# Attention and GLA jobs recut: 64-row products next to one another, softmaxes in pairs

## The chip, the cores and the metric

The kernel runs on one core of a Trainium2 chip. The core has a matrix engine (TensorE, in the profile PE, with its weight loads shown apart as PEld), three engines for elementwise work (VectorE or DVE, ScalarE or ACT, GpSimd or POOL), and a queue engine (SyncE, SP) that starts most transfers from the main memory. Each engine runs its own list of instructions in order, and lists wait for one another by semaphores. The metric is the device time of one execution in microseconds (us).

## The reference

Four transformer layers over 256 tokens of width 1024 in float32. The first two ("block 1", the same form twice) have a mixer with two attentions and a mixture of 16 experts; then a GLA layer and a differential attention layer ("block 2"), each with a larger mixture of 16 experts. What matters here, cut to the products that the change touches:

```
# block 1, global attention: 8 query heads, 2 key heads of 64
sc = einsum('bqgrd,bkgd->bgrqk', qi, k) * 64**-0.5 ; p = softmax(sc) ; o = p @ v
# block 1, dilated attention: 3 groups of 4 heads of 64, windows with dilation 1, 4, 16
sc = einsum('bqhd,bqkhd->bhqk', qi, kg) * scale + bias ; p = exp(sc - lse) ; o = p @ vg
# GLA: 4 heads, 4 chunks of 64 tokens, keys of 128, values of 256
state = dec[..., None] * state + k_c^T v_c ;  o = q_c state
# differential attention: 8 heads, two score sets of 64 rows each
w = softmax(q1 k1 + bias) - lam * softmax(q2 k2 + bias) ;  o = w @ v
```

## The kernel before

Each mixer is a `Flow` (a class of the kernel): projections by weight tiles of 256 columns, each split into a high and a low half (`whi` by ACT at L325, `wlo` by DVE at L335) and multiplied in three products, at L406, 48 matmuls to a `unit`. These fill PE from the start of a mixer to its end. Between them small tasks run as generators: after every 12 matmuls (`TICK`) `Flow.tick` lets each lane ("ada", "att", "scan", ...) take a step, and a task that yields n rests for n ticks. `width=2` lets two tasks of a lane be active at once. `drain` runs what is left of a lane without matmuls between the steps. What the generators write down is then put in order once more by a scheduler of the framework, which moves single instructions within an engine's list.

The tasks that matter:
- `global_job(tt, v)` (scores L1304, softmax L1307 to L1317, transposes L1326, values L1334): one block of 128 queries and one key head. The key head's 64 rows sit in partitions 0 to 63 or 64 to 127. A job makes the scores of four query heads on the same half of the rows, in two banks `s2`, one softmax after the other with a tick between, and transposes after three or four more ticks.
- `dil_job(tt, c)` (scores L1348 with 256 columns and L1353 in 64 x 64 pieces, softmax L1358 to L1366, transposes L1375, values L1383 and L1388): two heads, one on each half of the rows, again one after the other.
- `scan(h)` (state product `kv` at L1616, output product `po` at L1620, state update by DVE at L1625): one GLA head, four chunks, a step in each tick. `kv` contracts over the 64 rows of a chunk, rows 0 to 63 for even chunks, 64 to 127 for odd ones. `po` contracts over 128 rows and fills only 64 of the array's 128 columns. Heads 0 and 1 run side by side a tick apart, heads 2 and 3 later. `tail(h)` then normalises and transposes.
- `job(tt, hp)` of `diff` (scores L1751, softmax L1754 to L1762, transposes L1770, values L1780): two heads on the two halves of the rows, one after the other, with 128 or 256 keys.

A product of float32 operands is two passes on PE, so one such matmul of the program shows as x2 in the trace. In block 1 a lane "ada" also runs, whose DVE work (`adac`, L501) prepares later modulations and must be drained before `residual`, the last part of a mixer. `residual` is followed by `moe`, whose weight tiles are loaded into buffers that the mixer leaves.

Of the kernel before, what the change touches and what calls it, by code (L numbers as in the profile page):

```python
# [19 lines left out]
P = 128  # L20
# [84 lines left out]
def _plan(places, fixed):  # L105
# [9 lines left out]
          (3, 8, _plan([8, 9, 3, "r", 5] + ["r"] * 7 + [4, 6, 10, 7, "yy", 1, 2, 0, "sa", "rows"], FIX2), 14))  # L115
S_BANKS = 3
# [9 lines left out]
def body(ctx: ExitStack, tc: tile.TileContext, A: dict, out: bass.AP, dbg=None):  # L126
# [989 lines left out]
    def block1(l, prev):  # L1116

        with tc.tile_pool(name="gp", bufs=1, reuse_waits="tile") as gp:
            gates[l, 1] = gp.tile([P, D], F32, name="g2")
            es = gp.tile([P, 2, NE], F32, name="es")  # L1120
            with ExitStack() as stack:
# [26 lines left out]
                if prev is None:  # L1148
                    condR = d2.tile([P, KC, 32], F32, tag="pT", name="condR", bufs=4)
# [148 lines left out]
                def global_job(tt, v):  # L1298
                    hs = slice(64 * v, 64 * v + 64)
                    pr = []  # L1300
                    for c in range(2):
                        s2 = ps.tile([P, 2, 256], F32, tag="s2", name="s2", bufs=S_BANKS)
                        for j in range(2):
                            PE.matmul(s2[:, j, :], qT[hs, 2 * c + j, tt * P:(tt + 1) * P], kT[hs, :], start=True, stop=True,  # L1304
                                      skip_group_check=True)
                        nm = sm.tile([P, 2], F32, tag="nm", name="nm")
                        V.tensor_reduce(nm, s2, axis=AX.X, op=OP.max)  # L1307
                        sc = rq[:, tt, 4 * v + 2 * c:4 * v + 2 * c + 2]
                        V.scalar_tensor_tensor(nm, nm, -1.0, sc, op0=OP.mult, op1=OP.mult)
                        p = d2.tile([P, 2, 256], F32, tag="p", name="p", bufs=3)  # L1310
                        sums = sm.tile([P, 2], F32, tag="sums", name="sums")
                        for j in range(2):
                            S.activation(p[:, j], s2[:, j], AF.Exp, scale=sc[:, j:j + 1], bias=nm[:, j:j + 1],
                                         accum_out=sums[:, j:j + 1])
# [7 lines left out]
                    for p in pr:  # L1322
                        pT = d2.tile([P, 4, P], F32, tag="pT", name="pT", bufs=4)
# [7 lines left out]
                    for c, pT in enumerate(pTs):  # L1331
                        for kc in range(2):
                            for h in range(2):
                                PE.matmul(po[64 * h:64 * h + 64, c, :P], va[:, kc, 64 * v:64 * v + 64], pT[:, 2 * h + kc, :],  # L1334
                                          start=(kc == 0), stop=(kc == 1), tile_position=(0, 64 * h),
                                          skip_group_check=True)
                    yield 1
                    osl = (slice(None), slice(2 * v, 2 * v + 2), slice(tt * P, (tt + 1) * P))
# [3 lines left out]
                def dil_job(tt, c):  # L1342
                    pr = []
                    for hf in range(2):
                        hd = 2 * c + hf
                        s2 = ps.tile([P, 512], F32, tag="s2", name="s2d", bufs=S_BANKS)
                        hs = slice(64 * hf, 64 * hf + 64)
                        PE.matmul(s2[:, 0:256], qdT[hs, c, tt * P:(tt + 1) * P], kdT[hs, c, :],  # L1348
                                  start=True, stop=True, skip_group_check=True)
                        for g in (1, 2):  # L1350
                            for a in range(2):
                                ks = slice(tt * P + 64 * a, tt * P + 64 * a + 64)
                                PE.matmul(s2[64 * a:64 * a + 64, 192 + 64 * g:256 + 64 * g], qdT[hs, 2 * g + c, ks],  # L1353
                                          kdT[hs, 2 * g + c, ks], start=True, stop=True, tile_position=(64 * hf, 64 * a),
                                          skip_group_check=True)
                        slope = 2.0 ** (-8.0 * (hd + 1) / 12)
                        p = d2.tile([P, 384], F32, tag="p", name="pd", bufs=3)
# [3 lines left out]
                        V.tensor_tensor_reduce(p, s2[:, :384], p, 1.0, -3.0e38, OP.add, OP.max, mx)  # L1361
                        V.tensor_scalar(mx, mx, -1.0, None, op0=OP.mult)
                        su = sm.tile([P, 1], F32, tag="su", name="su")
                        S.activation(p, p, AF.Exp, bias=mx, accum_out=su)
                        V.reciprocal(su, su)
# [531 lines left out]
```

## Time and profile before

| what | value |
|---|---|
| median of 3 runs | 1644.25 us (1643.98 to 1645.04) |
| the profiled execution | 1644.99 us, span of its records 1643.2 us |
| PE busy in the span | 1464.9 us, 89% |
| DVE busy | 867.5 us, 53% |
| ACT busy | 430.3 us, 26% |
| mean granted clock of TensorE | 0.952 |

The span runs from the first to the last record of the profile; about 1.8 us of the execution lie outside it. Shares are means over stages of different kinds: the mixers lie at about 45 to 275 us, 447 to 670 us, 855 to 1000 us and 1250 to 1387 us, and the expert layers fill the rest.

### The profile page before, as it was taken

To read this page: it belongs to the slowest core of one execution; us is meant where nothing else is said; L and a number is where in the kernel's file an instruction comes from. 1 tells how busy PE (TensorE), PEld (TensorE's weight loads), DVE (VectorE), ACT (ScalarE), POOL (GpSimd) and SP (SyncE) were. 2 spreads that over 40 slices of the span, in tenths; PEclk is the share of its full clock that TensorE was granted. 3 is DMA by queue.
4 is the path that set the end of the run, shared out by engine and by line. 5 is a ranking of instruction groups with operands and counts; after the bars stand their busy time and mean duration, and the time that the engine had idled before them with its cause. 6 is when DMAs were issued, how large, how long until landed. Compare 5 with 4: busy or idle time off the path is not lost. (4 is left out here: it accounts for less than half of the span.)

```text
span 1643.2 us, 22584 instructions
## 1 busy us (share of the span) xinstructions
PE 1464.9 (89%) x9024; PEld 968.6 (59%) x9024; DVE 867.5 (53%) x1678; ACT 430.3 (26%) x729; POOL 132.9 (8%) x140
## 2 busy tenths in 40 slices
PE   4899997998699999599878998999898999999896
PEld 3788896443288899444447695443336988344332
DVE  3788898343798779524363574221126776122214
ACT  1453341111244433111125242010003552101000
POOL 0300002000130000200020001000002002000000
PEclk9999998999799999799989999999998999999898
DMA  9978699994775688899476387999989856999992
GB/s 307 365 245 282 202 312 352 340 308 165 248 252 171 205 294 251 240 367 358 156 241 199 104 290 256 375 376 366 360 306 296 272 204 240 359 367 387 334 387 104
DMA packets 324383, 461.80 MB, mean 281 GB/s; under 512 B 20077, under 2 KB 178285, under 8 KB 324258
## 3 DMA queue, kind: packets, MB, share of 16 engines
q1 hardware_dynamic: 308400, 445.29, 79.0%
q10 hardware_dynamic: 15858, 14.85, 3.5%
q8 instruction: 77, 1.26, 0.3%
q14 instruction: 48, 0.39, 0.1%
HBM read 456.43 MB, written 3.67 MB: 280 GB/s over the span
## 5 line engine op out<-in xcount | busy, mean ns | idle before, releaser
L763 PE MATMUL gu<-w,xg 128*64 128x512 f32 x1536 | 366.6, 597 | 7.3 <-ACT sa L796 6.5
L763 PEld LDWEIGHTS gu<-w,xg 128*64 128x64 f32 x1536 | 111.2, 137 | 218.9 <-issue 203.1
L817 PE MATMUL y<-w,sa 128*64 128x512 f32 x768 | 207.1, 596 | 1.1 <-DVE sa L801 1.1
L335 DVE TENSOR_TENSOR wlo<-w,whi 128x2048 fp32r<-128x2048 f32 (+2 forms) x92 | 183.4, 1997 | 45.3 <-ACT whi L325 42.4
L325 ACT ACTIVATE whi<-w 128x2048 fp32r<-128x2048 f32 (+2 forms) x92 | 157.7, 1726 | 141.0 <-PE acc L406 103.2
L828 DVE TENSOR_TENSOR yy<-y,yy 128x512 fp32r<-128x512 f32 x32 | 22.1, 692 | 197.3 <-ACT yy L827 197.3
L817 PEld LDWEIGHTS y<-w,sa 128*64 128x64 f32 x768 | 60.9, 137 | 107.4 <-issue 101.0
L501 DVE SCALAR_TENSOR_TENSOR adac<-w,ce,adac 128x512 f32<-128x512 f32 x140 | 104.5, 747 | 1.2
L313 PE MATMUL sc<-yy,st 128*128 128x512 f32 x256 | 87.2, 434 | 19.2 <-ACT yy L827 11.0
L313 PE MATMUL pg<-oh,zh 128*128 128x256 f32 x256 | 77.8, 332 | 25.3 <-DVEq L870 21.7
L406 PE MATMUL acc<-hh,whi 128*128 128x256 f32 x608 | 92.5, 294 | 1.7 <-ACT whi L325 1.7
L406 PE MATMUL acc<-hl,whi 128*128 128x256 f32 x608 | 93.0, 288 | 0.0
L827 ACT ACTIVATE yy<-y 128x512 fp32r<-128x512 f32 x32 | 19.1, 597 | 274.4 <-PE y L817 274.4
L406 PE MATMUL acc<-hh,wlo 128*128 128x256 f32 x608 | 87.1, 282 | 0.2 <-DVE wlo L335 0.2
L851 DVE TENSOR_TENSOR x<-x,sc 128x512 f32<-128x512 f32 x112 | 73.3, 681 | 22.0 <-PE sc L313 21.9
L406 PEld LDWEIGHTS acc<-hh,whi 128*128 128x128 f32 x608 | 80.0, 194 | 7.7 <-issue 4.7
L406 PEld LDWEIGHTS acc<-hl,whi 128*128 128x128 f32 x608 | 80.2, 191 | 4.8 <-issue 4.2
L313 PEld LDWEIGHTS pg<-oh,zh 128*128 128x128 f32 x256 | 58.3, 229 | 39.1 <-PEq L870 18.6
L189 POOL TENSOR_TENSOR rs<-ve,mhalf 128x1 f32<-128x1 f32 x24 | 25.3, 1055 | 678.7 <-DVE ve L188 678.7
L313 PEld LDWEIGHTS sc<-yy,st 128*128 128x128 f32 x256 | 42.0, 188 | 63.5 <-ACT yy L827 26.7
L406 PEld LDWEIGHTS acc<-hh,wlo 128*128 128x128 f32 x608 | 77.8, 188 | 2.2 <-issue 1.7
L823 DVE TENSOR_TENSOR yt<-y,g 128x512 f32<-128x512 f32 x32 | 22.0, 688 | 106.5 <-PE y L817 95.4
(375 smaller groups left out, 2196.9 us busy)
## 6 DMA issues: line engine op xcount, KB each, us to landing
w<-in_moe_w_gate_dram SPq DMA_DIRECT2D x64, 1024.0 KB, 12.1
w<-in_moe_w_up_dram SPq DMA_DIRECT2D x64, 1024.0 KB, 14.3
w<-in_moe_w_down_dram SPq DMA_DIRECT2D x128, 512.0 KB, 10.8
w<-in_w_ada_dram SPq DMA_DIRECT2D x47, 1024.0 KB, 6.5
w<-in_w_in_dram SPq DMA_DIRECT2D x40, 1024.0 KB, 6.6
w<-in_w_exp_gate_dram SPq DMA_DIRECT2D x64, 512.0 KB, 8.7
w<-in_w_exp_up_dram SPq DMA_DIRECT2D x64, 512.0 KB, 8.8
w<-in_w_exp_down_dram SPq DMA_DIRECT2D x64, 512.0 KB, 9.1
```

Source lines behind the costliest of these rows:

```text
L189: G.tensor_tensor(dst, ve, mhalf[:, :n], op=OP.pow)
L313: PE.matmul(dst, l, r, start=(i == 0), stop=(i == n - 1), skip_group_check=True)
L325: S.activation(hi[:, k0:k0 + n], w, AF.Copy)
L335: eng.tensor_tensor(lo[:, k0 + x:k0 + y], w[:, x:y], hi[:, k0 + x:k0 + y].bitcast(F32), op=OP.subtract)
L406: PE.matmul(dst, l, r, start=(start and i == 0), stop=(i == n - 1), skip_group_check=True)
L501: V.scalar_tensor_tensor(acc, ws[k // 4][:, k % 4], ce[:, k:k + 1], acc, op0=OP.mult, op1=OP.add)
L763: PE.matmul(gu[64 * j:64 * j + 64, :], xg[:, 4 * kh + k, (2 * pr + j) * CAP:(2 * pr + j + 1) * CAP], ws[j][:, k, :], start=(kh == 0 and k ...
L817: PE.matmul(y[64 * j:64 * j + 64, :], aT[:, f, 64 * j:64 * j + 64], w[:, j, k, :], start=(f == 0), stop=(f == NF - 1), tile_position=(0, 6 ...
L823: V.tensor_tensor(yt[:, hs], y, gate[:, hs], op=OP.mult)
L827: S.activation(yh[:, hs], src, AF.Copy)
L828: V.tensor_tensor(yl[:, hs], src, yh[:, hs].bitcast(F32), op=OP.subtract)
L851: V.tensor_tensor(X[:, tt, hs], X[:, tt, hs], sc, op=OP.add)
```

## The change

The jobs are cut along other lines, so that a product on rows 0 to 63 stands next to one on rows 64 to 127, and in the GLA a product on columns 0 to 63 next to one on columns 64 to 127.
- `global_job` takes a pair of query heads `c` for both key heads instead of four query heads of one key head. The four score products alternate between the halves and between two banks. Both softmaxes' exponentials come before both normalisations, and one wait of four ticks (`SM_TICKS`) stands where there were waits of 1, 1 and 3. A pause of two ticks (`JOB_GAP`) stands between the first two jobs of the lane.
- `dil_job` and `job` write both heads' scores first, alternating the halves, then both softmaxes, then wait four ticks.
- `scan(ha)` runs two heads with the second one chunk behind, in six steps of two ticks.
- The softmax tiles `p` get 4 buffers instead of 3, the transposed tiles `pT` 3 instead of 4.

The number of products, of softmax and of copy instructions stays the same. The core of the diff:

```diff
+SM_TICKS = 4
+JOB_GAP = 2
+P_BUFS = 4
...
-                def global_job(tt, v):
-                    hs = slice(64 * v, 64 * v + 64)
+                def global_job(tt, c):
+                    s2 = [ps.tile([P, 2, 256], F32, tag="s2", name="s2", bufs=S_BANKS) for _ in range(2)]
+                    for j in range(2):
+                        for v in range(2):
+                            hs = slice(64 * v, 64 * v + 64)
+                            PE.matmul(s2[v][:, j, :], qT[hs, 2 * c + j, tt * P:(tt + 1) * P], kT[hs, :], start=True, stop=True,
+                                      skip_group_check=True)
                     pr = []
-                    for c in range(2):
-                        s2 = ps.tile([P, 2, 256], F32, tag="s2", name="s2", bufs=S_BANKS)
-                        for j in range(2):
-                            PE.matmul(s2[:, j, :], qT[hs, 2 * c + j, tt * P:(tt + 1) * P], kT[hs, :], start=True, stop=True,
-                                      skip_group_check=True)
+                    for v in range(2):
...
+                        pr.append((p, sums))
+                    for p, sums in pr:
                         V.reciprocal(sums, sums)
                         for j in range(2):
                             V.tensor_scalar(p[:, j], p[:, j], sums[:, j:j + 1], None, op0=OP.mult)
-                        pr.append(p)
-                        yield 1
-                    yield 3
+                    yield SM_TICKS
...
-                        fl.add("att", *[global_job(tt, v) for tt in range(2) for v in range(2)], width=2)
+                        fl.add("att", global_job(0, 0), pause(JOB_GAP), global_job(0, 1), global_job(1, 0), global_job(1, 1), width=2)
...
-            def scan(h):
+            def scan(ha):
+                heads = (ha, ha + 1)
+                po = {h: ps.tile([P, 2, 256], F32, tag="s2", name="po", bufs=3) for h in heads}
+                for m in range(6):
+                    kv = {}
+                    for h in heads:
+                        n = m - (h - ha)
+                        if 0 <= n < 4:
...
+                            PE.matmul(kv[h][:, :256], kt[rows_, n // 2, h * P:(h + 1) * P], v[rows_, n // 2, h * 256:(h + 1) * 256],
+                                      start=True, stop=True, skip_group_check=True)
...
+                    yield 2
...
-            fl.add("scan", scan(0), scan(1), width=2)
+            fl.add("scan", scan(0), width=2)
...
-                fl.add("scan", scan(2 + u))
+                if u == 1:
+                    fl.add("scan", scan(2))
```

What the scheduler makes of it is seen in PE's list. In the first mixer, at the first global job (`s_843`, `s_870` and so on are score banks, L1304 the score products, L406 the projections), the list before has two products to a bank, each bank on one half of the rows:

```order
L1304 MATMUL s_843<-kT,qT 128x256 x2
L406 MATMUL acc<-hl,whi 128x256 x4
L406 MATMUL acc<-hh,wlo 128x256 x8
L1304 MATMUL s_870<-kT,qT 128x256
L1291 MATMUL ptq<-consts,qro 128x128 x4
L1304 MATMUL s_870<-kT,qT 128x256
L1304 MATMUL s_883<-kT,qT 128x256 x2
```

In the changed program (where all lines of the code stand 3 or more further down) the same place on PE reads:

```order
L1307 MATMUL s_843<-kT,qT 128x256
L1307 MATMUL s_844<-kT,qT 128x256
L1307 MATMUL s_843<-kT,qT 128x256
L1307 MATMUL s_844<-kT,qT 128x256
L409 MATMUL acc<-hl,whi 128x256 x4
L409 MATMUL acc<-hh,wlo 128x256
```

The first job's four products now alternate between a bank of one half and a bank of the other, without a projection between them.

In the GLA, on PE, at the second to fourth chunk of the first heads (`kv` state products, `po` output products, one chunk and one head each), before:

```order
L1616 MATMUL kv<-vg,kq 128x256
L1620 MATMUL po<-st,kq 64x256
L1616 MATMUL kv<-vg,kq 128x256
L1620 MATMUL po<-st,kq 64x256
L406 MATMUL acc<-whi,hl_10488 128x256 x4
L406 MATMUL acc<-wlo,hh_10487 128x256 x8
L1616 MATMUL kv<-vg,kq 128x256
L1620 MATMUL po<-st,kq 64x256
```

And in the changed program at that place:

```order
L1628 MATMUL kv<-vg,kq 128x256 x2
L1634 MATMUL po<-st,kq 64x256 x2
L409 MATMUL acc<-whi,hl_10488 128x256 x4
L409 MATMUL acc<-wlo,hh_10487 128x256 x8
L409 MATMUL acc<-whi,hh_10487 128x256 x8
L409 MATMUL acc<-whi,hl_10488 128x256 x4
```

Two heads' state products stand together, and behind them two heads' output products; the next such group comes 24 projections later.

At the end of the differential attention, on PE, where the last job's scores (`s2f`), transposes (`ptf`) and value products (`podf`) meet the first products of `residual` (`oh`, `ol` are the heads' outputs), before:

```order
L1751 MATMUL s2f<-kq 128x256 x2
L406 MATMUL acc<-wlo,oh_15539 128x256 x6
L406 MATMUL acc<-whi,oh_15539 128x256 x6
L406 MATMUL acc<-whi,ol_15540 128x256 x6
L406 MATMUL acc<-wlo,oh_15539 128x256 x6
L1770 MATMUL ptf<-consts,pbuf 128x128
L1780 MATMUL podf<-vb,wT 128x128
L1770 MATMUL ptf<-consts,pbuf 128x128 x3
```

And in the changed program, from the last scores on:

```order
L1766 MATMUL s2f<-kq 128x256 x4
L409 MATMUL acc<-whi,hl_15538 128x256 x4
L409 MATMUL acc<-wlo,hh_15537 128x256 x8
L409 MATMUL acc<-whi,oh_15539 128x256 x6
L409 MATMUL acc<-whi,ol_15540 128x256 x6
L409 MATMUL acc<-wlo,oh_15539 128x256 x6
L409 MATMUL acc<-whi,oh_15539 128x256 x6
L409 MATMUL acc<-whi,ol_15540 128x256 x6
L1791 MATMUL ptf<-consts,pbuf 128x128 x2
L409 MATMUL acc<-wlo,oh_15539 128x256 x6
L1801 MATMUL podf<-vb,wT 128x128 x2
L1791 MATMUL ptf<-consts,pbuf 128x128 x4
```

Between the last scores and the transposes of the last job stand 48 projections where there were 24.

## Rows read from the trace of the kernel before

**Rows 1.** The page, busy us, share of the span and instructions of each engine.

```profile
PE 1464.9 (89%) x9024; PEld 968.6 (59%) x9024; DVE 867.5 (53%) x1678; ACT 430.3 (26%) x729; POOL 132.9 (8%) x140
```

**Rows 2.** Busy us by stretch of the mixers: stretch, length, engines, granted clock, DMA.

```profile
82.00:205.00 123.00, 121.27 (x958) 104.91 (x957) 105.64 (x206) 50.74 (x86) 0.00 (x0) 0.95 0.73 243
205.00:246.00 41.00, 38.90 (x311) 38.33 (x311) 37.95 (x67) 17.28 (x22) 0.00 (x0) 0.96 0.97 313
500.00:617.00 117.00, 116.79 (x1007) 106.51 (x1006) 93.98 (x189) 53.23 (x89) 0.00 (x0) 1.00 0.70 232
905.00:950.00 45.00, 45.00 (x259) 31.54 (x258) 25.42 (x39) 12.90 (x12) 2.10 (x3) 1.00 0.37 120
1276.00:1348.00 72.00, 72.00 (x556) 66.08 (x555) 53.73 (x183) 44.79 (x107) 4.16 (x6) 1.00 0.68 221
```

**Rows 3.** The longest wait of PE from 82 to 246 us: total, times, longest.

```profile
PE acc L406 <- ACT mh L1458: 2.1, 1, 2.1
```

**Rows 4.** Timeline of PE, first global job: start, us, line, operation, shape, records.

```profile
83.94 1.13 PE L1304 MATMUL s<-kT,qT 64*128 64x256 f32 x4
85.00 0.74 PE L406 MATMUL acc<-hl,whi 128*128 128x256 f32 x4
...
87.83 1.13 PE L1304 MATMUL s<-kT,qT 64*128 64x256 f32 x6
88.89 1.21 PE L406 MATMUL acc<-hh,whi 128*128 128x256 f32 x8
```

**Rows 5.** PE busy (records) of the global scores L1304 alone, by mixer.

```profile
82.00:205.00 123.00, 8.60 (x32) 4.98 (x32) 0.95 0.73 243
500.00:617.00 117.00, 6.79 (x32) 4.09 (x32) 1.00 0.70 232
```

**Rows 6.** Timeline of PE, dilated scores of two heads.

```profile
124.24 0.70 PE L1348 MATMUL s2d<-kdT,qdT 64*128 64x256 f32 x2
124.86 0.45 PE L1353 MATMUL s2d<-kdT,qdT 64*64 64x64 f32 x8
```

**Rows 7.** PE busy of the dilated scores in the second mixer, L1348, then L1353.

```profile
500.00:617.00 117.00, 5.57 (x16) 2.35 (x16) 1.00 0.70 232
...
500.00:617.00 117.00, 3.58 (x64) 2.48 (x64) 1.00 0.70 232
```

**Rows 8.** PE busy in the GLA, of `kv` L1616, then of `po` L1620.

```profile
905.00:950.00 45.00, 11.14 (x32) 4.71 (x32) 1.00 0.37 120
...
905.00:950.00 45.00, 10.33 (x32) 3.06 (x32) 1.00 0.37 120
```

**Rows 9.** Timeline of PE in the GLA, one `po` run.

```profile
916.40 0.65 PE L1620 MATMUL po<-st,kq 128*64 128x256 f32 x2
```

**Rows 10.** The page, costliest group: expert products on alternating column halves.

```profile
L763 PE MATMUL gu<-w,xg 128*64 128x512 f32 x1536 | 366.6, 597 | 7.3 <-ACT sa L796 6.5
```

**Rows 11.** PE busy of the differential scores L1751.

```profile
1276.00:1348.00 72.00, 12.39 (x64) 7.84 (x64) 1.00 0.68 221
```

**Rows 12.** Timeline of PE, four differential score products, 128 and 256 keys.

```profile
1280.93 1.14 PE L1751 MATMUL s2f<-kq 64*128 64x128 f32 x8
```

**Rows 13.** Timeline of PE, end of the differential attention, with idle time and releaser.

```profile
1350.96 0.33 PE L1770 MATMUL ptf<-consts,pbuf 128*128 128x128 f32 x1 [1.17 <-DVE pbuf L1762]
1352.23 0.41 PE L1770 MATMUL ptf<-consts,pbuf 128*128 128x128 f32 x2 [0.94 <-DVE pbuf L1762]
```

**Rows 14.** Busy us of one stretch of the first mixer, columns as in rows 2.

```profile
160.00:170.00 10.00, 10.00 (x62) 7.07 (x61) 4.63 (x15) 1.73 (x6) 0.00 (x0) 0.56 0.37 133
```

**Rows 15.** Softmax of a global job: groups by tile (min/median/max ns), then by line (mean).

```profile
L1313 ACT ACTIVATE p<-s,nm,rq x32: 546/560/566, 90.2 to 530.7; 128x256 f32<-128x256 f32 x32
...
L1307 DVE TENSOR_REDUCE nm<-s x16: 668/681/693, 88.7 to 526.3; 128x2 f32<-128x512 f32 x16
...
L1317 DVE TENSOR_SCALAR p<-p,sums 128x256 f32<-128x256 f32 x16 | 4.9, 346 | 0.0
```

**Rows 16.** Lines of DVE from 82 to 250 us.

```profile
L335 DVE TENSOR_TENSOR wlo<-w,whi 128x2048 fp32r<-128x2048 f32 (+2 forms) x24 | 44.0, 1841 | 6.7 <-ACT whi L325 6.5
```

More of the change, by code (lines that the diff above doesn't have):

```diff
@@ L1493, in bias_task @@
         yield 1
-        fsb = pool.tile([8, 384], F32, tag="pT", name="fsb", bufs=4)
+        fsb = pool.tile([8, 384], F32, tag="pT", name="fsb", bufs=3)
         V.tensor_copy(fsb, pf[0:8, :384])
@@ new lines, in scan @@
+            def scan(ha):
[6 more added lines that the diff above has]
+                        if 0 <= n < 4:
+                            rows_ = slice(64 * (n % 2), 64 * (n % 2) + 64)
+                            kv[h] = ps.tile([P, 512], F32, tag="acc", name="kv", bufs=3)
+                            PE.matmul(kv[h][:, :256], kt[rows_, n // 2, h * P:(h + 1) * P], v[rows_, n // 2, h * 256:(h + 1) * 256],
+                                      start=True, stop=True, skip_group_check=True)
+                    for h in heads:
+                        n = m - (h - ha)
+                        if 0 < n < 5:
+                            i, par = n - 1, (n - 1) % 2
+                            PE.matmul(po[h][64 * par:64 * par + 64, i // 2, :], qT[:, h, i * 64:(i + 1) * 64], st[i % 2][:, h],
+                                      start=True, stop=True, tile_position=(0, 64 * par), skip_group_check=True)
+                    for h in heads:
+                        n = m - (h - ha)
+                        if n == 0:
+                            V.tensor_copy(st[0][:, h], kv[h][:, :256])
+                        elif 0 < n < 4:
+                            V.scalar_tensor_tensor(st[n % 2][:, h], st[(n + 1) % 2][:, h], dec[:, h, n:n + 1], kv[h][:, :256],
+                                                   op0=OP.mult, op1=OP.add)
+                    yield 2
+                for h in heads:
+                    o = og[:, h]
+                    S.activation(o, po[h], AF.Copy)
+                    sq = d2.tile([P, 2, 256], F32, tag="hf", name="sq2", bufs=1)
+                    ss = sm.tile([P, 2], F32, tag="ssd", name="ssg")
+                    V.tensor_tensor(sq, o, o, op=OP.mult)
+                    V.tensor_reduce(ss, sq, axis=AX.X, op=OP.add)
+                    rs2 = sm.tile([P, 2], F32, tag="rsg", name="rsg", bufs=4)
+                    rstd_of(rs2, ss, LN_EPS, 2, 1.0 / 256)
+                    for tt in range(2):
+                        V.scalar_tensor_tensor(o[:, tt], o[:, tt], rs2[:, tt:tt + 1], gn[:, h * 256:(h + 1) * 256], op0=OP.mult, op1=OP.mult)
+                    os[h] = o
+                    yield 1
@@ L1742, in job @@
                 pair = pairs.pop(0)
+                s2 = [ps.tile([P, 512], F32, tag="s2", name="s2f", bufs=S_BANKS) for _ in range(2)]
+                for i in range(2):
+                    for hf in range(2):
+                        rows_ = slice(64 * hf, 64 * hf + 64)
+                        PE.matmul(s2[hf][:, i * 256:i * 256 + nk], qT[hp][rows_, i, tt * P:(tt + 1) * P], kT[hp][rows_, i, :nk],
+                                  start=True, stop=True, skip_group_check=True)
                 for hf in range(2):
                     h = 2 * hp + hf
-                    rows_ = slice(64 * hf, 64 * hf + 64)
-                    s2 = ps.tile([P, 512], F32, tag="s2", name="s2f", bufs=S_BANKS)
                     p = pbuf[:, pair[hf]]
@@ L1750, in job @@
                     for i in range(2):
[L1751 to L1754 removed]
+                        V.tensor_tensor_reduce(p[:, i, :nk], s2[hf][:, i * 256:i * 256 + nk], Tb[h // 4][:, h % 4, 256 - nk:256], 1.0, -3.0e38,
                                                OP.add, OP.max, mx[:, i:i + 1])
@@ L1758, in job @@
                         S.activation(p[:, i, :nk], p[:, i, :nk], AF.Exp, bias=mx[:, i:i + 1], accum_out=su[:, i:i + 1])
+                    ws.append((p, su))
+                for p, su in ws:
                     V.reciprocal(su, su)
```

90 lines of the change are left out of this document (30 added, 60 removed).

## The prediction

> **What bounds the kernel now.** I read the page's engine table first: PE is busy 89% of the span, DVE 53%, ACT 26% [rows 1]. Such a mean hides the stages, so next came the busy time of each engine in the stretches of the mixers where the changed jobs run [rows 2]. There PE stands at 121.27 of 123 us, 116.79 of 117, 45.00 of 45 and 72.00 of 72: in these stretches the time is PE's list, and a microsecond taken out of it is a microsecond of the kernel, as long as the engine behind it keeps up. Third I read PE's waits. Over both stretches of the first mixer the longest costs 2.1 us [rows 3]; none has to do with the products that are recut. DVE is second: 86% in the first stretch, 93% in the next (37.95 of 41), 80% in the second mixer, 56% in the GLA, 75% in the differential attention [rows 2]. So only the first mixer has an engine close behind PE.
>
> Last I read what a product over half the array costs. A float32 product is two passes, two records. Two global score products on one half of the rows take 1.13 us from the first start to the last end, and the next run begins 1.06 after it (83.94 to 85.00). The run at 87.83 holds six records, three products, one of them on the other half; it takes the same 1.13, and again 1.06 to the next run [rows 4]. So a product on rows 0 to 63 and one on 64 to 127 do run at once. One score product alone takes 0.70, 0.62 to the next run [rows 6]. All prices below follow: one step of two passes 0.70, two steps 1.13; every run overlaps the next by 0.07 (1.13 less 1.06).
>
> **The change part by part, in PE's busy time.** The number of products stays; the steps shrink where opposite halves stand together.
>
> Global scores. Now 8.60 us in the first mixer and 6.79 in the second [rows 5]. In the changed list the first mixer has three groups of four products that alternate, and the last job's four cut into two runs of two on one half each: 5 runs x 1.13 = 5.65, a saving of 2.95. The second has three such groups and two runs of one pair: 3 x 1.13 + 2 x 0.70 = 4.79, saving 2.00.
>
> Dilated scores. In the second mixer 5.57 + 3.58 = 9.15 us [rows 7]. All four jobs stand paired there: 0.70 for the two large products, and for the 64 x 64 pieces, now eight products in a run where a run of four takes 0.45 [rows 6], between 0.45 (a run twice as full costs the same) and 0.90 (no gain). The trace shows no such run; I take 0.60, nearer to the rows on which opposite halves overlap. 4 x 1.30 = 5.20 saves 3.95, bounds 2.75 to 4.55. In the first mixer two of the four jobs stand paired; by the same 1.0 a job, 2.0.
>
> Scan. `kv` takes 11.14 and `po` 10.33 us for 16 products each [rows 8], so 0.70 and 0.65 apiece. The changed list has `kv` as 5 pairs and 6 single ones, since the second head runs one chunk behind: 11 x 0.70 = 7.7, saving 3.4. `po` lies on column halves: 6 pairs and 4 single ones. A lone run takes 0.65 [rows 9]. What a pair on column halves gives is read from the expert products, alternating column halves, two passes of 512 columns: 366.6 us for 1536 records, 239 ns each [rows 10], where a pass of 256 columns alone already takes 0.22 (the 0.43 between 1.13 and 0.70, halved). So column halves overlap nearly fully, a pair costs about 0.70, and 4 x 0.65 + 6 x 0.70 = 6.8 saves 3.5. Were column halves not to overlap here, nothing of this 3.5 comes.
>
> Differential scores. 12.39 us [rows 11] in 13 runs of all forms. The changed list has eight groups of four, half of them with 128 keys. A run with two 128-key products on one half and two 256-key ones on the other took 1.14 [rows 12]. So a 256-key group costs 1.13. A 128-key group does half of that, 0.70, and 1.13 at the worst. 4 x 0.70 + 4 x 1.13 = 7.3 saves 5.1 (3.4 at the worst).
>
> These sum to 2.95 + 2.00 + 3.95 + 2.0 + 3.4 + 3.5 + 5.1 = 22.9 us. But busy time of a run contains the 0.07 that the next run overlaps: some 28 runs fewer give back 28 x 0.07 = 2.0. Remain 20.9.
>
> End of the differential attention. Here PE waits 1.17 and 0.94 us for the last softmaxes [rows 13]. The changed list puts 24 more projections ahead of the transposes. One takes (1.21 - 0.74) / 4 = 0.12 us [rows 4], so 2.8 us more cover, against which the joint softmax is later by one softmax's rest. I count a gain of 2, bounds 0 and 3.
>
> Waits that the joint softmax brings. A global job's pair needs maximum 0.68 twice, four exponentials of 0.56, four multiplications of 0.35 [rows 15]; these add to 5.0, and overlap of ACT and DVE brings the chain to about 4.8. Ahead of the transposes stand 52 to 105 projections, 6.2 to 12 us. The least margin is 1.4 us, less than one weight split of DVE (1.84 [rows 16]). Behind a waiting transpose stand all later projections, and behind these the split buffers. Bounds 0 and 4; I count 1.
>
> First mixer. DVE is so near its limit [rows 2] that part of the 4.95 us saved there ends as a wait for splits instead. The wait of 2.1 us [rows 3] shows that this happens today. I count half lost, 2.5; bounds 0 and 5.
>
> Clock. The granted clock is 1.00 in all the stretches but the first mixer's. There it falls to 0.56 in one stretch of 10 us [rows 14], close to the lower level of 1.2 GHz, while the list is dense with transposes and small products. At the full clock these 10 us would be 5.6, so 4.4 to win at most. In the changed list projections stand between those products. Bounds: 4.4 lost once more elsewhere and 4.4 won. I count 1 won.
>
> Copies, softmax and DMAs keep their numbers. One buffer fewer for `pT`, one more for `p`: the DMA of the bias task that takes a `pT` buffer must also wait for DVE, on ACT's queue, behind which ACT's casts stand; the table's use is over 500 us later, so nothing.
>
> Sum: 20.9 + 2 - 1 - 2.5 + 1 = 20.4 us, from the profiled execution's 1645.0 (span 1643.2): 1624.6. The median of the runs shown lies 0.7 lower, so 1623.9: **1624**.
>
> **Rivals.** *DVE becomes the bound in the first mixer and later the split paces PE elsewhere too.* For it: 93% in one stretch. Against: 56% to 80% in the others. All 4.95 of the first mixer go, and a quarter of the other 18: 1624 + 2.5 + 4.5 = 1631. A sentence of the Trainium skill stands beside it (TensorEngine Tiling (Array Packing), section "PSUM Bottleneck"): tiling speeds up the matrix engine but not the emptying of its results. By that rule alone the DVE-bound first mixer gives nothing, which the trace neither shows nor excludes.
>
> *A product's two passes start strictly in the program's order.* Then the second half's first pass can begin only with the first half's second, and every group lasts one pass longer, 0.22 us; with about 27 groups 5.9 us, so 1630. Against it: the six records in the time of four [rows 4] would then take 1.35. The Trainium skill says so (TensorE: Matmul & The Clock Gate, section "Part 3: Packing small matmuls — row/col tiling"): products start and end in program order without reordering. By the rule it is 1630, by the row 1624; the row decides for me.
>
> *Slower: PE blocks at the joint transposes.* Before, the first softmax's transposes needed one softmax through; now both must be. If DVE takes three splits of 1.84 in between, the chain is 4.8 + 5.5 = 10.3 us against leads of 6.2 to 12. Jobs with short leads, some 12 of 24, then wait 2 us each, 24 us in all: 1648. It decides from a chain of 8.3 us on, that is two foreign splits. For it: DVE's load in the first mixer. Against: its 56% to 80% elsewhere, and most leads are longer.
>
> *The pairs don't overlap in the new order* (results go to other banks, weights change each time): only the end and the fewer runs are left, about 1642. Rows 4 speak against it.
>
> *Better: the clock stays up and all bounds go well.* Clock 4.4, no loss on DVE 2.5, no waits 1, end 1 more, small products 0.9: 3.4 + 2.5 + 1 + 1 + 0.9 = 8.8, so 1615.
>
> **How the numbers follow.** Chances: the forecast's case 0.52, DVE as the bound 0.18, order of passes 0.10, blocked transposes 0.07, no overlap 0.05, better 0.08. The range takes in the better case and the two dearer ones with their spread, 1613 to 1636; outside lie the last two cases and the tails. A measurement of this kernel can tell about 0.2%, 3.3 us, from no change. Faster holds all but blocked transposes and half of the no-overlap case: 0.89; same 0.05; slower 0.06.
>
> **What would show it.** Right: a first-job run of eight score records of about 1.13 us, `kv` pairs of 0.70, and PE busy in the five stretches shorter by some 21 us in sum, while the expert layers stay. The order of passes shows as 1.35 for such a run and 0.9 for `kv` pairs. DVE as the bound shows as waits of projections for `wlo` in the first mixer; the blocked transposes as PE's idle time ahead of `ptp`, `ptd` and `ptf`. The forecast is wrong if a run of eight records takes about 2 us, or if over 8 us of new PE idle time appear.

## The result and the profile after

| | median | runs | ratio to the kernel before |
|---|---|---|---|
| before | 1644.55 us | 1643.98 to 1645.04 | |
| after | 1622.38 us | 1619.32 to 1625.64 | 0.9859, 95% interval 0.9842 to 0.9876 |
| forecast | 1624 us | range 1613 to 1636 | |

The kernel became 22.2 us faster, 1.4%. The profiled execution of after took 1619.32 us, its span is 1617.5, 25.7 shorter than that of before. The first part of the page (busy us, share of the span, instructions) answers to [rows 1]:

```profile
PE 1435.8 (89%) x9024; PEld 953.5 (59%) x9024; DVE 864.3 (53%) x1678; ACT 428.6 (26%) x729; POOL 131.4 (8%) x140
```

PE has as many instructions as before and 29.1 us less busy time. The same five stretches as in [rows 2], cut at about the same places in the program (engines PE, PEld, DVE, ACT, POOL, then granted clock, DMA share, GB/s). The cuts are rounded, so that lengths are compared only in the table further down:

```profile
84.00:198.00 114.00, 113.33 (x966) 101.70 (x964) 103.46 (x205) 50.41 (x86) 0.00 (x0) 0.99 0.77 253
198.00:242.00 44.00, 39.48 (x311) 38.27 (x310) 40.39 (x71) 17.34 (x22) 0.00 (x0) 0.96 0.92 307
495.80:607.00 111.20, 110.31 (x1009) 102.76 (x1008) 93.81 (x190) 52.46 (x89) 0.00 (x0) 1.00 0.73 239
886.00:925.00 39.00, 39.00 (x283) 32.24 (x281) 21.66 (x28) 13.62 (x11) 1.40 (x2) 1.00 0.45 157
1256.00:1324.00 68.00, 67.67 (x552) 63.15 (x551) 53.71 (x187) 44.87 (x114) 4.16 (x6) 1.00 0.74 247
```

PE still fills its stretches. Now the recut products alone, as PE busy time (records) by stretch: the global scores (answering to [rows 5]), the dilated scores in 256 columns and in 64 (first and second mixer each, [rows 7]), `kv` and `po` ([rows 8]), the differential scores ([rows 11]):

```profile
84.00:198.00 114.00, 5.66 (x32) 0.99 0.77 253
495.80:607.00 111.20, 4.81 (x32) 1.00 0.73 239
...
84.00:198.00 114.00, 4.19 (x16) 0.99 0.77 253
495.80:607.00 111.20, 2.87 (x16) 1.00 0.73 239
...
84.00:198.00 114.00, 3.36 (x64) 0.99 0.77 253
495.80:607.00 111.20, 1.85 (x64) 1.00 0.73 239
...
890.00:945.00 55.00, 7.87 (x32) 1.00 0.50 172
...
890.00:945.00 55.00, 6.50 (x32) 1.00 0.50 172
...
1256.00:1324.00 68.00, 7.80 (x64) 1.00 0.74 247
```

And PE's timeline (start, us, line, operation, records). A run of eight records is four products, two on each half; four records are two products:

```profile
87.09 1.13 PE L1307 MATMUL s<-kT,qT 64*128 64x256 f32 x8
...
546.39 0.70 PE L1352 MATMUL s2d<-kdT,qdT 64*128 64x256 f32 x4
547.02 0.46 PE L1358 MATMUL s2d<-kdT,qdT 64*64 64x64 f32 x16
...
908.44 0.70 PE L1628 MATMUL kv<-vg,kq 64*128 64x256 f32 x4
909.07 0.65 PE L1634 MATMUL po<-st,kq 128*64 128x256 f32 x4
...
1315.33 0.71 PE L1766 MATMUL s2f<-kq 64*128 64x128 f32 x8
...
1317.81 1.13 PE L1766 MATMUL s2f<-kq 64*128 64x256 f32 x8
```

Four products take what two took [rows 4], two take what one took [rows 6, 9].

For the rest of this text the program is cut at the same instructions of PE's list in every kernel, and a stretch is the time from PE's start of the one to its start of the other, added up from the timeline. "First mixer" runs from the first projection to the products of `residual`, "second mixer" from a projection just ahead of its first global job into its `residual`, "scan" from the GLA's last projections before it to the experts, "end" is the last job of the differential attention and its `residual`. Where a stretch takes in `residual`, it runs up to the routing and the experts' first gather products (`pg`):

| stretch, us | before | after |
|---|---|---|
| first mixer | 201.6 | 196.5 |
| second mixer | 163.8 | 158.0 |
| GLA ahead of the scan | 43.2 | 40.6 |
| scan | 105.7 | 98.0 |
| differential attention | 95.2 | 91.7 |
| its end | 48.4 | 47.1 |
| all else | 985.4 | 985.6 |

(All else is what is left of the span: 1643.2 and 1617.5.) The gain lies where the jobs were recut. In the same way, start to start, the recut products hold PE for 21.9 us less: global 14.4 to 9.8, dilated 17.4 to 10.7, `kv` 10.0 to 7.1, `po` 9.2 to 5.8, differential 11.5 to 7.2.

### The profile page after: what moved, and what is told of

It is laid out like the page before. It is cut to its first block, busy times and chain, and to the rows that moved or that the text cites. A ratio compares the mean times of both kernels' runs of the same rounds, so it can differ in the third digit from the quotient of the medians.

```text
span 1617.5 us, 22578 instructions
## 1 busy us (share of the span) xinstructions
PE 1435.8 (89%) x9024; PEld 953.5 (59%) x9024; DVE 864.3 (53%) x1678; ACT 428.6 (26%) x729; POOL 131.4 (8%) x140
## 5 line engine op out<-in xcount | busy, mean ns | idle before, releaser
L854 DVE TENSOR_TENSOR x<-x,sc 128x512 f32<-128x512 f32 x112 | 73.3, 681 | 22.1 <-PE sc L316 21.9
```

The lines of the kernel that those rows point to most:

```text
L854: V.tensor_tensor(X[:, tt, hs], X[:, tt, hs], sc, op=OP.add)
```

## Experiments

Times are medians. The kernel before stood at 1644.4 to 1645.6 beside them. Totals of the changed program spread by 6 to 11 us between executions, but for one that is named, so that a few us are read from a stretch of the profile and not from the total.

**The changed kernel again.**

> The changed kernel once more, unchanged. Its four times spread from 1619.3 to 1625.6 us, where the kernel before spread by 1.1. Theory: the saved products are the same in every execution, so the score products, kv and po keep their PE busy time (5.7, 4.8, 7.8, 7.1 to 7.8 and 5.8 to 6.4 us), and what varies is the clock and the waits of the start and of the first mixer. Rival: the pairs overlap in some executions only; then the PE busy time of the score products differs from the first profile by over 1 us. Median between 1619 and 1625.

1620.15 us by the median of all six executions. One of them took 6154 us; why is not known. The other five have a median of 1617.97 us (1615.47 to 1624.87), ratio 0.9836 (0.9814 to 0.9859), and from here on this is what is called the second measurement of the changed kernel. All the recut products lie within 0.03 us of the first profile. What differs is elsewhere: the GLA ahead of the scan took 43.0 us where the first profile has 40.6, with a granted clock of 0.91 over 20 us (first line, this run) where the first profile has 1.00 (second fence), and two expert stages took 0.9 and 2.4 us more.

```profile
865.00:885.00 20.00, 19.79 (x130) 17.24 (x130) 9.84 (x7) 14.66 (x18) 0.00 (x0) 0.91 0.51 160
```

```profile
865.00:885.00 20.00, 19.19 (x136) 16.65 (x137) 10.69 (x7) 16.12 (x19) 0.00 (x0) 1.00 0.52 161
```

So the 2.6 us of that stretch in the table are not the change's.

**Order inside the groups.** The loops over halves and over products change places:

```diff
-                    for j in range(2):
-                        for v in range(2):
+                    for v in range(2):
+                        for j in range(2):
```

> The groups of scores are written with both products of one half first and then both of the other (A A B B in place of A B A B), in the global, the dilated and the differential attention; neighbours stay neighbours. Theory N (neighbours): PE takes up the other half's product as soon as its rows are free, whatever the order inside the group; runs of eight records stay at 0.71 (128 keys) and 1.13 us, the time stays within 2 us of the changed kernel, 1622. Rival A (alternation): products start in order, so the second A has to begin before the first B; a group takes three product times in place of two, +0.43 for each of some 10 groups of 256 columns, +0.22 for 4 of 128, about +0.5 for each of 6 dilated jobs: 4.3 + 0.9 + 3 = +8.2 us, 1630.5, and the runs of eight at 1.56.

1621.79 us, ratio 0.9858 (0.9836 to 0.9879). In the global scores and the differential ones order costs nothing; in the dilated ones everything that the pairing had brought is gone. (The list did run in the new order: in single records of the trace the other half's first product starts 13 ns behind the first one of the run at 495.63, and 7 ns behind it in the changed kernel.)

```profile
495.63 1.14 PE L1307 MATMUL s<-kT,qT 64*128 64x256 f32 x8
...
545.99 0.70 PE L1352 MATMUL s2d<-kdT,qdT 64*128 64x256 f32 x2
546.62 0.45 PE L1357 MATMUL s2d<-kdT,qdT 64*64 64x64 f32 x8
547.00 0.70 PE L1352 MATMUL s2d<-kdT,qdT 64*128 64x256 f32 x2
547.62 0.45 PE L1357 MATMUL s2d<-kdT,qdT 64*64 64x64 f32 x8
```

Neither theory holds alone: N where two products of a half stand in a row, A where five do. The second mixer takes 161.7 us, 3.7 more, about what four dilated jobs lose (2.08 from 545.99 to the last end, in place of 1.09 each).

**Small products half by half.** To see why:

```diff
-                    for g in (1, 2):
-                        for a in range(2):
-                            for hf, hs in enumerate(rows_):
+                    for hf, hs in enumerate(rows_):
+                        for g in (1, 2):
+                            for a in range(2):
```

> The dilated scores in the order A256 B256, then four small products of half A, then four of half B. In the second run the order with five products of A ahead of five of B took 2.08 us for 20 records in place of 1.04, while A A B B in the other attentions took no more than A B A B. Theory W (PE finds the other half's product only if it stands no more than two or so products behind): the eight small ones run one after the other, a run takes about 0.7 + 0.9 = 1.5 us. Rival C (a full-width product of half B could not start beside small ones, whose columns are halves; small ones beside small ones can): 1.04 to 1.1 us, as in the changed kernel.

```profile
544.77 0.70 PE L1352 MATMUL s2d<-kdT,qdT 64*128 64x256 f32 x4
545.40 0.47 PE L1358 MATMUL s2d<-kdT,qdT 64*64 64x64 f32 x16
```

1622.47 us, one run. Four small products of one half, then four of the other: they overlap fully, 1.10 us for the job. So W falls: PE finds a partner four products behind. What the run before lacked fits C: there the first product of the other half was a wide one behind small ones that each fill half the columns. C is not shown by itself. In the run before five products of a half stood ahead of the other half's, here four, so that a reach of PE which ends between four and five would fit both runs as well.

**Both heads of the scan on the same chunk.**

```diff
-                        n = m - (h - ha)
+                        n = m
```

> The GLA's two heads run on the same chunk in place of one chunk apart: two kv products stand together on the same half of the rows, two po products on the same half of the columns. The same neighbours, even fewer interruptions of the projections, but no opposite halves. Theory (halves): a kv pair takes 1.13 in place of 0.70 us, a po pair about 1.08 in place of 0.65; kv 7 x 1.13 + 2 x 0.70 = 9.3 against 7.7, po about 8.6 against 6.5, less some 0.8 for fewer interruptions: +3 us, about 1625 if the changed kernel stands at 1622. Rival (grouping): the GLA's gain came from standing in groups and breaking the projections less often; then it is 1 us faster than the changed kernel, 1621, and kv and po together take no more PE time than in it.

1623.64 us, ratio 0.9870 (0.9850 to 0.9889). `kv` and `po` by busy time in the scan, then two of its pairs in the timeline:

```profile
880.00:945.00 65.00, 9.29 (x32) 1.00 0.54 184
...
880.00:945.00 65.00, 8.62 (x32) 1.00 0.54 184
```

```profile
901.50 1.13 PE L1628 MATMUL kv<-vg,kq 64*128 64x256 f32 x4
902.56 1.08 PE L1634 MATMUL po<-st,kq 128*64 128x256 f32 x4
```

As the theory of halves had it (9.3 and 8.6). The scan's stretch is 102.7 us, 4.7 more than changed and 3.0 less than before: standing together is worth something, the halves are worth more. Of the 3.0 us, 2.5 are `kv` and `po` themselves: start to start `kv` goes from 10.0 to 8.65 and `po` from 9.2 to 8.06, since a run's first product costs 0.63 and a second one behind it only 0.43. The projections around them give some 0.6 (71.3 us before, 70.7 here).

**One part undone at a time.** The edits put back the functions of the kernel before, for the first two mixers' jobs, for the scan, for the differential attention's jobs; a line of each:

```diff
-                def global_job(tt, c):
+                def global_job(tt, v):
...
-            fl.add("scan", scan(0), width=2)
+            fl.add("scan", scan(0), scan(1), width=2)
...
-                yield SM_TICKS
+                    yield 1
+                yield 3
```

> The changed kernel with the global and dilated jobs of the first two mixers as before; GLA and differential attention recut. Theory (each part saves in its own stretch, by its own products): the first two mixers take as long as before (first 141, second 164 us, where the changed kernel takes 136.5 and 158), GLA and differential attention as long as changed (98 and 92): 10 to 11 us slower than the changed kernel, 1631 to 1633. Rival (the gain is one of clock and waits that come and go): the second mixer stays within 2 us of the changed kernel's.

> The changed kernel with the GLA's scan as before. Theory (own products): kv 10.0 and po 9.2 us in place of 7.1 and 5.8 by the time from start to start, the scan's stretch at 105.5 in place of 98, 7.5 us slower, 1628 to 1630; the score products and all other stretches as in the changed kernel. Rival (the forecast's price of 0.70 for a po pair was right, and the rest of the gain in the stretch came from the clock): po returns by 2.5 us only and the stretch by 5.

> The changed kernel with the differential attention's jobs as before. Theory (own products; at the end the waits only moved): the scores at 11.5 in place of 7.2 us, the stretch up to the last job's values at 95.1 in place of 91.7, its end at 48.4 in place of 47.1: 4.5 us slower, 1625 to 1627. Rival (the longer cover of 24 more projections is worth the 2 us that were forecast for the end): the end alone at 49 or more.

| stretch, us | before | after | mixers' jobs old | scan old | diff. jobs old |
|---|---|---|---|---|---|
| first mixer | 201.6 | 196.5 | 198.7 | 196.2 | 195.7 |
| second mixer | 163.8 | 158.0 | 163.7 | 157.6 | 157.6 |
| scan | 105.7 | 98.0 | 97.7 | 105.7 | 98.0 |
| differential attention | 95.2 | 91.7 | 91.8 | 91.8 | 95.1 |
| its end | 48.4 | 47.1 | 47.2 | 47.6 | 48.7 |
| median of the runs | 1644.55 | 1622.38 | 1627.93 | 1624.53 | 1623.02 |

In the second mixer, the scan and the differential attention each part gives its own stretch back to within 0.3 us and moves none of the others by more than 0.5: with the scan old, `kv` and `po` stand at 11.14 and 10.33 us busy, the numbers of [rows 8]. Measured from the changed kernel's first median, the totals moved by less than I had expected (5.6, 2.2 and 0.6 us, against 10, 7.5 and 4.5), and from its second by about as much (10.0, 6.6 and 5.1). The two medians of the same program lie 4.4 us apart, so the totals decide nothing here. The first mixer is the exception: its old jobs cost 2.2 us there, not 5.

**One tick less of cover.**

```diff
-SM_TICKS = 4
+SM_TICKS = 3
```

> The changed kernel with three ticks in place of four between both softmaxes and the transposes, 12 projections or 1.4 us less cover. It puts the forecast's slower case to the test (PE blocks at the joint transposes). Theory (cover is ample, chain about 4.8 us): PE's waits ahead of ptp, ptd and ptf stay under 2 us in sum, the time within 3 us of the changed kernel. Rival (the cover is just enough in the changed kernel): most of 24 jobs wait over 0.7 us, 15 to 25 us slower, above 1635.

1623.93 us, ratio 0.9886 (0.9855 to 0.9916). PE waits 0.3 us ahead of `ptf` and nothing that shows ahead of `ptp` and `ptd`. The forecast's slower case is out. What it costs lies elsewhere: the differential attention takes 94.4 us, 2.7 more. PE waits there four times ahead of value products and `pto`, 1.2 us in all (0.2 in after), and its projections are cut into 31 pieces in place of 25; how much of the rest the pieces cost was not tried by itself.

**DVE's load in the first mixer.**

```diff
-            V.scalar_tensor_tensor(acc, ws[k // 4][:, k % 4], ...)
+            if step == 1 or k % 4 == 0: V.scalar_tensor_tensor(acc, ws[k // 4][:, k % 4], ...)
```

> In the first mixer only, the modulation task leaves out six of its eight terms (the output is then not the reference's; its weights are still loaded): some 72 DVE instructions of 0.75 us less, 53 us of DVE work less in the first mixer. Theory (DVE paces the merge stage of the first mixer, 207 to 232 us, and took back what the products saved): PE's waits there for mt (2.3 us) go and the waits for mh (2.1) and behind (1.9, 2.2) shrink: 2 to 6 us faster than the changed kernel, 1616 to 1620. Rival (the waits are ACT's or the latency of the chain's): no more than 0.5 us faster.

The total, 3116.49 us, says nothing: the modulations are other ones, and the stages behind the first mixer take twice the time (probably because the tokens go to other experts; not looked into). The first mixer can still be compared, since its instructions but those left out are the same. It took 179.3 us against 196.5, and its `residual` 41.1 against 49.2. The longest waits of PE from 84 to 280 us (total, times, longest), in after:

```profile
PE pos L707 <- DVE r_m L540: 4.1, 1, 4.1
PE ptq L1294 <- DVE qro L1288: 2.7, 1, 2.7
PE acc L409 <- DVE wlo L338: 2.2, 1, 2.2
PE acc L409 <- ACT mh L1465: 2.1, 1, 2.1
PE accb L409 <- DVE mt L1463: 2.0, 2, 1.5
PE acc L409 <- DVE ot L975: 1.9, 1, 1.9
```

and in this run, where all but the first are gone and that one is shorter:

```profile
PE pos L707 <- DVE r_m L540: 2.3, 1, 2.3
PE rp L1002 <- ACT hTr L996: 1.2, 2, 1.0
PE pg L316 <- DVE oh L723: 1.0, 1, 1.0
PE pa L511 <- DVE pTd L1383: 0.7, 1, 0.7
```

I had expected 2 to 6 us, since I counted only the four waits that begin with `wlo`. It is 25. By PE's list, start to start, 14 of the 25 us are waits of PE (8 of them those four), about 8 are projections that took less time, at a somewhat higher granted clock (0.99 over the mixer in place of 0.97), and 2.7 are recut products, because all jobs stand paired in this list. So DVE's work costs this mixer waits, but not all of the 25 us are waits for DVE.

**The same work on PE.** A generator like the existing tile at the kernel's start makes eight of the twelve modulation tiles; its core:

```diff
+        for k in range(KC):
+            for j in range(4):
+                PE.matmul(pa[32 * j:32 * j + 32, :128], cond[:, k, :], ws[k // 4][:, k % 4, j * 128:(j + 1) * 128],
+                          start=(k == 0), stop=(k == KC - 1), tile_position=(0, 32 * j), skip_group_check=True)
```

> The changed kernel, and in the first mixer 8 of the 12 modulation tiles are made by PE (32 products of 32 columns each, as at the kernel's start) in place of 8 DVE instructions of 0.75 us each: some 45 us of DVE work less in the first mixer, PE some 6 to 8 us more there (0.05 us for a pass, 64 passes, a transposition, less the 1.04 us of the products that go). Theory (DVE paces the first mixer): the fourth run, with 53 us of DVE work less, was shorter by 25 us from the mixer's start to its end; here 18 to 21 come back less 7: 11 to 14 us faster than the changed kernel, 1607 to 1611. Rival (PE paces it, and the fourth run was faster because its DVE results were not needed or came with other work): the 7 us of PE work are paid, 1628.

> The kernel before, with the same 8 modulation tiles made by PE: the recut's worth without DVE's load is the difference between this run and the fifth. Theory (DVE took back part of the recut in the first mixer: 2.3 us of waits, and two dilated jobs and a global one left unpaired): the difference is larger than the 22 to 25 us between the two kernels, by 3 to 5: 26 to 29. Rival (DVE's limit and the recut have nothing to do with each other): the same 22 to 25.

With the recut 1616.26 us, ratio 0.9825 (0.9809 to 0.9841), the fastest version here and faster than both kernels by median. Whether it beats the changed kernel is not shown by the totals: its interval stands clear of the first measurement's by 0.0001 and overlaps with the second's, whose median, 1617.97, is 1.7 us away. From the first projection to the end of `residual` it takes 238.8 us against 245.6, 6.9 less before rounding, and some 6 less than the mean of five profiles with the same first mixer (244.9; 243.4 to 245.6). I had expected 11 to 14. Part of what is missing is PE's price: start to start the eight tiles' products hold it for 15 us, 1.9 a tile, and with what they replace PE has some 9 us more to do, where I had put 6 to 8. All dilated jobs but one now stand paired in the first mixer's list, without any change to them.

With the kernel before 1637.98 us, 0.9965 (0.9949 to 0.9980). The difference of the two is 21.7 us, not the 26 to 29 that I expected from a recut freed of DVE. In the first mixer the recut is worth 204.2 - 198.4 = 5.8 us with DVE relieved, at the same granted clock of 0.98 in both profiles, and 201.6 - 196.5 = 5.1 without.

**A later split at the end.**

```diff
-        fl.ahead(into=hold())
+        hold_rest = fl.ahead(into=hold(), whole=False)
...
+            if u == 1:
+                hold_rest()
```

> The changed kernel, with DVE's low half of the last weight tile (hold, 2.29 us) made after the second unit of residual in place of before it. Theory (at the end of the differential attention PE waits for DVE's normalisation, which stands behind this split): the waits of 1.8 us ahead of pto shrink to under 0.5, the stretch of 47.1 us to 45.5, the kernel is 1 to 2 us faster, 1618 to 1621. Rival (the waits are the latency of the chain of products, copies and GpSimd's root): the wait stays over 1.3 us and the time is the same.

1636.37 us, 0.9952 (0.9938 to 0.9965): 14 us slower than the changed kernel, a plain miss. The wait ahead of `pto` shrank (1.1 us in place of 1.6), but in all four mixers' ends PE then stood before the late split itself, for 6.0, 1.8, 3.3 and 3.8 us, together about the 14 that were lost. The first one:

```profile
247.04 2.07 PE L409 MATMUL acc<-hold,mh 128*128 128x256 f32 x8 [5.99 <-DVE hold L338]
```

## Why the prediction was right

1623.9 was forecast and 1622.4 came, well inside the range, and for the reason given: opposite halves of the array overlap, and the mixers' time is PE's list. That it came within 1.5 us is in part luck: by the second measurement it is 1618.0, 6 us below the forecast and still inside the range. By the steps of the sum, in PE busy time:

| step | forecast | measured |
|---|---|---|
| global scores, first and second mixer | 2.95 + 2.00 | 2.94 + 1.98 |
| dilated scores, second mixer | 3.95 (2.75 to 4.55) | 9.15 - 4.72 = 4.43 |
| dilated scores, first mixer | 2.0 | 10.55 - 7.55 = 3.0 |
| `kv` | 3.4 | 11.14 - 7.87 = 3.27 |
| `po` | 3.5 | 10.33 - 6.50 = 3.83 |
| differential scores | 5.1 | 12.39 - 7.80 = 4.59 |
| fewer runs' overlap | -2.0 | 24.0 by busy time, 21.9 start to start: -2.1 |
| sum | 20.9 | 21.9 |

The global scores came to the hundredth: a run of eight records is one of four. Mis-sized were these:
- *The small dilated products.* I put 0.60 between 0.45 and 0.90 and wrote that no row shows such a run. Sixteen records take 0.46: all four quarters of the array work at once. The lower bound was the value.
- *First mixer's dilated jobs.* The 3.0 are not all pairing. Before, the same products took 9.15 us in the second mixer and 10.55 here. Of these 1.4 us, 0.8 are the low clock of [rows 14] (a run of two wide products took 1.22 in place of 0.70 there, one of small ones 0.69 in place of 0.45), and 0.6 are two runs of small products that other work cut in two. So 0.8 of the 3.0 came back with the clock, and recutting gave 2.2 where I had 2.0. The row for 256 columns, in the columns of [rows 7] (for 64 it has 4.46):

```profile
82.00:205.00 123.00, 6.09 (x16) 0.95 0.73 243
```

- *`po`.* I took 0.70 for a pair, from products of 512 columns; it is 0.65, as for one alone, so nothing is paid for the second.
- *Differential scores.* Two of the four groups with 256 keys take 1.25 and 1.42 in place of 1.13; the profile names no wait there.
- *The end.* The 24 more projections ahead of the transposes are 18 for the first two transposes (42 stand ahead of them) and 24 for the rest (48). The step said a gain of 2, bounds 0 and 3; it gave 1.3. The waits of [rows 13] are gone, as forecast, and others have come in their place. PE's timeline at the end of after, with idle time and releaser:

```profile
1324.00 0.38 PE L1791 MATMUL ptf<-consts,pbuf 128*128 128x128 f32 x2
...
1326.03 0.71 PE L1801 MATMUL podf<-vb,wT 128*128 128x128 f32 x4 [0.93 <-ACT wT L1793]
1326.57 0.60 PE L1791 MATMUL ptf<-consts,pbuf 128*128 128x128 f32 x4
1327.49 1.16 PE L1801 MATMUL podf<-vb,wT 128*128 128x128 f32 x8 [0.31 <-ACT wT L1793]
...
1330.97 0.56 PE L1819 MATMUL pto<-consts,odf 128*128 128x128 f32 x2 [1.62 <-DVE odf L1813]
```

The 24 projections that now cover the softmax are missing behind it, and the chain from the last transposes to `pto` lies bare. DVE's timeline shows what it did when `odf` was due, the split of a tile (`hold`) that PE takes up only at 1337.59:

```profile
1325.85 2.29 DVE L338 TENSOR_TENSOR hold<-w,hold 128x2048 fp32r<-128x2048 f32 x1
1328.06 0.42 DVE L1808 TENSOR_TENSOR sq<-odf 128x256 f32<-128x256 f32 x1
```

- *Waits of the joint softmax.* Counted 1 us. PE waits for none of the transposes but one (0.2 ahead of `ptf`), and five times ahead of value products, for the transposes' copies, 2.2 us in all, 1.2 of them in the two waits at the end shown above (before: four times, 1.3 us, and 0.8 ahead of `ptd`). The run with a tick less of cover shows that there was room ahead of the transposes.
- *First mixer, DVE and clock.* I had DVE take back half, 2.5 us. New waits of 2.3 us for the merge of the two attentions (`mt`) stand in after, about that. The clock, of which I had counted 1 of 4.4 us, came back whole where the granted clock before was 0.56 [rows 14]:

```profile
154.00:164.00 10.00, 10.00 (x109) 7.84 (x109) 7.79 (x26) 4.14 (x8) 0.00 (x0) 1.00 0.71 230
```

But part of it was lost again near the mixer's start, where after ran at the lower clock (same columns, before and then after):

```profile
31.00:52.00 21.00, 18.89 (x224) 16.02 (x225) 11.22 (x16) 8.56 (x12) 4.19 (x6) 0.92 1.07 366
31.00:52.00 21.00, 17.93 (x198) 15.67 (x199) 11.15 (x19) 8.94 (x11) 2.81 (x6) 0.76 1.07 366
```

Over the whole first mixer PE spent some 17 us at the lower of its two levels (1.2 GHz) in the profile of before and some 14 in that of after. The 3.4 us less are worth about 1.7 at twice the clock, so the term of 1 was about right, and the clock is not most of the 5.1. With the mixers' jobs old the slow stretch was there again, at 0.72 (same columns, that run), and the start ran at 0.92:

```profile
160.00:170.00 10.00, 10.00 (x73) 7.57 (x73) 7.47 (x25) 1.98 (x6) 0.00 (x0) 0.72 0.66 223
```

That profile has some 14 us at the lower level too, as many as after, and is 2.2 us longer. From before to after PE's list in this mixer gives, start to start: recut products 5.5 us less (0.8 of it clock), the transposes and value products behind them 4.1 less (before, most of what they lost stood in the slow stretch), projections 2.8 more (the slow start), modulation products 0.6 more, waits 1.3 more; these give 4.9 of the 5.1. So the terms for this mixer, 4.95 saved, 2.5 to DVE and 1 from the clock, each came near what was put; their sum, 3.5, was short by 1.6. That is no more than the spread of single profiles, since five with the same first mixer lie between 194.3 and 196.5 us. No run held the clock fixed, and whether the new list itself keeps the later stretch at the full clock stays open.

Of the rivals, the strict order of passes is out: by it four products in the order A A B B take at least 1.56 us, and they took 1.14. The Trainium skill (TensorE: Matmul & The Clock Gate, "Part 3: Packing small matmuls — row/col tiling") says that products start and end in program order, without reordering; the measurement decides against it here.

DVE as the bound of the first mixer is not borne out either: by it that mixer would have gained nothing, and it gained 5.1 us, 5.8 with DVE relieved. DVE's work does cost it waits, by the run with the light modulations; no run relieved DVE in another stage. Beside this rival the prediction named the Trainium skill (TensorEngine Tiling (Array Packing), "PSUM Bottleneck"): tiling speeds up TensorE but not the emptying of its results. No run here tests that sentence by itself.

## What to carry to other kernels

A product that uses half of the array's rows or columns costs nothing if one of the other half stands near it in PE's list (here a lone one and a pair both took 0.70 us): price a recut by the runs in the trace where this already happens by accident, and take the list after scheduling to count which groups stay together. When an engine is bound, look at what a second engine is given in the same stretch: here 45 us of DVE work that PE does in 15 (9 more than it had there) made the first mixer another 6 to 7 us shorter, though the total does not show it clear of the spread. Work that covers one wait is taken from behind it; ask what lies bare there.

## Not expected of the hardware

- Four 64 x 64 products on four quarters of the array run at once: sixteen records in 0.46 us, where eight on one half of the rows took 0.45. A lone one (two records) takes 0.32.
- Products of the two halves overlap even where the list does not alternate them: A A B B takes 1.14 us like A B A B, four small A ahead of four small B overlap fully (0.47), yet a wide B behind small A does not (2.08 against 1.09 for a job).
- Projections took a little more time where more products cut into them, but the number of pieces alone does not give it: in the scan's stretch 562 of their passes held PE for 70.9 us in 23 pieces before and for 69.7 in 19 after, and for 70.1 in 17 with both heads on the same chunk.
- How long PE stands at its lower clock changes between lists and between executions: in the first mixer the stretch from 150 to 172 us had a granted clock of 0.77 before and 0.84 with the mixers' jobs old, and 1.00 in both profiles of the changed kernel, while the stretch from 31 to 52 us had 0.76 and 0.92 in those two.
